# Seven block products for the up projections of a two-layer encoder, and one modulation computed in another place

## The chip, the cores and the metric

The kernel runs on one core of a Trainium2 chip. The core has engines with a queue of their own each: TensorE (PE, the matmuls; PEld is its loading of stationary operands), VectorE (DVE), ScalarE (ACT), GpSimd (POOL) and SyncE (SP), whose queue issues all transfers of this kernel. Matmul results land in PSUM, eight banks of 128 partitions x 512 float32; everything else lies in SBUF. The metric is the device time of one execution in microseconds (us), the median of several runs.

## The reference

Two sequences (a prompt of 256 tokens and a sample of 512) go through the same trunk of two layers, width 1024. Each layer has a mixer (layer 0: a matrix LSTM in both directions; layer 1: sliding-window attention) and a gated feed-forward with a convolution of three taps along the tokens. All of it is float32.

```python
for l in range(DEPTH):
    mod = jax.nn.silu(c) @ adaln_w[l] + adaln_b[l]          # 1024 -> 6 x 1024
    sh1, sc1, g1, sh2, sc2, g2 = [t[:, None, :] for t in jnp.split(mod, 6, axis=-1)]
    h = rmsnorm(x, norm_g[l, 0]) * (1 + sc1) + sh1
    y = mlstm_mixer(h, ...) if l % 2 == 0 else swa_mixer(h, ...)
    x = x + g1 * y
    h = rmsnorm(x, norm_g[l, 1]) * (1 + sc2) + sh2
    x = x + g2 * conv_ffn(h, ffn_w_up[l], ffn_conv_w[l], ffn_conv_b[l], ffn_w_down[l])
return rmsnorm(x, final_g)

def conv_ffn(h, w_up, conv_w, conv_b, w_down):
    u = h @ w_up                                            # 1024 -> 2 x 2816
    u = depthwise_conv3(u, conv_w) + conv_b
    return (jax.nn.silu(u[..., :2816]) * u[..., 2816:]) @ w_down
```

## The kernel before

Activations are kept transposed: channels on partitions (eight chunks of 128), the 768 tokens of both sequences on the free axis. Every float32 operand is split into a rounded high part and the rest (`fp_copy_split`, L166: ACT writes the high part at L170, DVE the low one at L171), and a product is three matmuls: high x high, high x low, low x high.

**Weights** come in units of 1 MB (`load`, L177), through two buffers with the tag `raw`; a unit is cut into two halves of 1024 columns, and each is split into `whi` and `wlo` (three buffers each). The matrices of the modulation come through the same two `raw` buffers.

**The program** is written in the order in which the work depends on each other, and a planner puts it on the queues: a list per engine, in which an instruction that isn't ready can be passed by a later one, and in which tiles of one tag take their buffers in turn. PSUM is three rotating banks `ps` (projections) and five rotating banks `pa` (norms, attention, down projections).

**Stages.** The first normalizations and layer 0's first modulation; mixer 0 (`mlstm`, L447), whose projections are followed by calls of `step` (L193); the output projection of the mixer with the residual (`out_proj`, L434), the sample's 512 tokens first and then the prompt's 256; feed-forward 0 (`ffn`, L834); mixer 1 (`swa`, L647); its output projection; feed-forward 1 with the final normalization.

**`step`** takes one piece from the generator `fill`. In mixer 0 this is a chain of the second and third part of layer 0's modulation (`adaln`, L292): eight pieces each, one transfer of 1 MB and its matmuls on PE to a piece. `step` is called once after the first window of mixer 0 (L218), after each of the seven further query and key projections, after the four value projections and after the four units of the output gate. A loop behind the mixer runs what is left. In feed-forward 0 `fill` is layer 1's modulation (`adaln_v`, L350): six groups of four transfers; for each transfer DVE makes four operations over 1024 columns that sum into one buffer `ada` (L364 and L366), and a group ends with four small matmuls with ones (they sum over the partitions), two copies and four transposes.

**A feed-forward** goes through 11 parts of 256 hidden channels. `up(p)` has two units (gate and value) of two halves; each half is 24 matmuls for the sample's 512 tokens and 24 for the prompt's 256 (`gemmT`). `conv` (L838) reads the result from PSUM: ACT does the middle tap with the bias (L841), DVE the outer two (L843, L844). Then Silu on ACT (L856), the product on POOL (L866), and the split of the product. `down(p)` runs after `up(p + 1)`: eight output chunks x two sequences x six matmuls into `pa`, and the residual update on DVE (L432).

**Norms** (`Norm`, L59) collect squares on ACT and their sum on POOL while the residual is updated; two later stages are put between other products by `tick`, and `ready` forces them. The first three halves of a feed-forward run as a `window`: one token range of 256 after the other, so that the products of the first ranges lie beside the norm of the last.

Of the kernel before, what the change touches and what calls it, by code (L numbers as in the profile page):

```python
# [13 lines left out]
P = 128  # L14
D = 1024
KC = D // P
T = 768
SEQS = ((0, 512), (512, 768))
# token ranges that are normalized on their own: (first, last, sequence)
SAMPLE, PROMPT = (0, 512, 0), (512, 768, 1)  # L20
RANGES = ((0, 256, 0), (256, 512, 0), PROMPT)
# [9 lines left out]
# column offsets inside the packed per-partition parameter block  # L31
# [11 lines left out]
# column offsets inside the block of shape constants  # L43
# [6 lines left out]
# weight unit indices  # L50
# [7 lines left out]

class Norm:  # L59
# [3 lines left out]
    def __init__(self, net, xt, rng, apply, pool_adds=True):  # L63
        self.net, self.xt, self.rng, self.apply = net, xt, rng, apply
# [16 lines left out]
    def stages(self):  # L81
# [17 lines left out]
        for c in range(KC):  # L99
            self.apply(c, self.x(c), pr, self.rng)  # L100
# [8 lines left out]
class Net:  # L109
    def __init__(self, tc, ctx, io):  # L110
# [8 lines left out]
        self.dp = pool("scratch", space=bass.MemoryType.DRAM)  # L119
        self.n = 0  # L120
# [26 lines left out]

    def ps(self):
        return self.psp.tile([P, 512], F32, tag="ps", name=self.nm("ps"), bufs=3)

    def pa(self):
        return self.psp.tile([P, 512], F32, tag="pa", name=self.nm("pa"), bufs=5)
# [13 lines left out]
    def fp_copy_split(self, hi, lo, src, scale=None):  # L166
        """hi = round(src * scale), lo = src * scale - hi"""
# [50 lines left out]
    def window(self, items):  # L218
        """several weight halves, one token range after the other"""
# [19 lines left out]
    def gemmN(self, u, evac):  # L239
        """tokens on partitions, 256 output columns on the free axis"""  # L240
# [15 lines left out]
    def setup(self):  # L256
# [19 lines left out]
        self.hh = self.hp.tile([P, KC, T], R, name="hh")  # L276
        self.hl = self.hp.tile([P, KC, T], R, name="hl")
# [72 lines left out]
    def adaln_v(self, l, pool):  # L350
        """the same with the sums over k of the rows of one partition on the vector engine"""
# [82 lines left out]
    def out_proj(self, u0, act, xt, l):  # L434
        for rng in (SAMPLE, PROMPT):
            norms = [Norm(self, xt, r, self.modulated(l, 1)) for r in RANGES if r[2] == rng[2]]
            for u in range(4):
                for h, w in self.halves(u0 + u):
                    c = 2 * u + h
                    self.resid(xt, self.gemmT(w, rng[2], act), l, 16, c, rng)  # L440
                    for n in norms:
                        n.square(c)
            for n in norms:
                self.start(n.rng, n.stages())

# [1 line left out]
    def mlstm(self, pool, gw, xt):  # L447
        nc, io = self.nc, self.io
        T6 = T // P
        # gates: rows 0-3 / 32-35 hold the forward / backward heads  # L450
# [57 lines left out]
        for h in range(4):  # L508
            # M along the free axis on all partitions, and its diagonal blocks masked
# [23 lines left out]
            # values, with two columns of ones for the normalizer  # L533
# [11 lines left out]
            # transposed scores: keys on partitions, queries on the free axis  # L545
# [86 lines left out]
        # output gate  # L632
# [14 lines left out]
    def swa(self, pool):  # L647
# [6 lines left out]
        def halves2(o, hh, ll, p0):  # L654
            """both partition halves of hh / ll from the 64 rows at p0"""
# [42 lines left out]
        # every row repeated, so that a row pitch of 511 reads it shifted by one per partition  # L698
# [135 lines left out]
    def ffn(self, l, xt, pool, apply, keep=None):  # L834
# [3 lines left out]
        def conv(ps, u, ch, s0, s1):  # L838
            n = s1 - s0
            w = lambda tap: self.cst(CW + (l * 44 + ch) * 3 + tap)  # L840
            nc.scalar.activation(u[:, s0:s1], ps, AF.Identity, bias=self.cst(CB + l * 44 + ch), scale=w(1))  # L841
            stt = nc.vector.scalar_tensor_tensor
            stt(u[:, s0 + 1 : s1], ps[:, : n - 1], w(0), u[:, s0 + 1 : s1], ALU.mult, ALU.add)  # L843
            stt(u[:, s0 : s1 - 1], ps[:, 1:], w(2), u[:, s0 : s1 - 1], ALU.mult, ALU.add)  # L844

        def up(p):
            g = self.slab([P, 2, 2, T], R)
            gs = {}

            def gate(c):  # L850
# [239 lines left out]
```

## Time and profile before

| | us |
|---|---|
| median of 3 runs | 1968.58 (1967.79 to 1971.22) |
| the profiled execution, from its first to its last instruction | 1968.9 |
| PE busy | 1890.1 |
| DVE busy | 1184.6 |
| ACT busy | 726.6 |
| POOL busy | 300.1 |
| moved by DMA | 188.63 MB, 96 GB/s on average |

A page of the profile gives busy times per engine, the span in slices, the chain of work that ended last, and the costliest groups of instructions. A group's row reads: line, engine, operation, what it writes <- what it reads, shape, number; then busy time in us and the mean of one in ns; then the idle time ahead of these on their engine and what ended it. In a timeline the first two numbers are start and duration in us. In a table of stretches each engine has its busy time and in brackets its instructions; the last three columns are the clock granted to PE, the share of DMA and GB/s. Matmuls overlap in PE's pipeline, so the duration of one is longer than the distance from one to the next.

### The profile page before, as it was taken

Reading aid. Unit: us, or ns where it says so; the run is one execution under the profiler, and the core shown is the slowest. Engines: PE = TensorE matmul, PEld = TensorE weight load, DVE = VectorE, ACT = ScalarE, POOL = GpSimd, SP = SyncE. Lnnn points to the kernel's source line nnn. Section 1 sums busy time; section 2 is a strip of 40 time slices with the busy share of each in tenths; the row PEclk is TensorE's granted clock in tenths of the full one; section 3 lists DMA queues with packets and bytes.
Section 4 is the critical chain, followed back from the end, with each engine's and each line's share of the span. In section 5 each row is a group of like instructions: output and inputs, shape, how many; then the busy total and the mean of one; then the engine's idle time right before and its main releaser. Section 6 shows DMA issues by size and latency. Waiting matters only on the chain.

```text
span 1968.9 us, 28848 instructions
## 1 busy us (share of the span) xinstructions
PE 1890.1 (96%) x11636; PEld 1638.4 (83%) x11636; DVE 1184.6 (60%) x2217; ACT 726.6 (37%) x1411; POOL 300.1 (15%) x336
## 2 busy tenths in 40 slices
PE   6799999999999999999999959999999999999997
PEld 2698898878988888888888858778988888888886
DVE  4534344323887778878556836785755555555556
ACT  3444344433442222222223526674532222222222
POOL 5111101223110000000002102243110000000003
PEclk9899999999999999999999979999999999999998
DMA  8313213243243233333112561123211111111111
GB/s 319 124 40 114 96 65 123 68 157 125 102 149 129 98 133 113 128 121 137 65 65 88 84 122 60 38 86 109 99 52 65 65 65 65 65 65 65 65 43 65
DMA packets 48609, 188.63 MB, mean 96 GB/s; under 512 B 3863, under 2 KB 21527, under 8 KB 33116
## 3 DMA queue, kind: packets, MB, share of 16 engines
q1 hardware_dynamic: 48476, 186.79, 28.7%
q8 instruction: 92, 1.51, 0.3%
q14 instruction: 41, 0.34, 0.1%
HBM read 176.17 MB, written 10.60 MB: 95 GB/s over the span
## 4 chain that ended last, share of the span: by engine, by line
PE 87%; DVE 5%; DMA 5%; ACT 1%; POOL 1%; issue 1%; SPq 0%; POOLq 0%; DVEq 0%; ACTq 0%
PE ps L164 58%; PE pa L164 27%; DMA bdiag<-bs 2%; PE pa L786 1%; DMA slab<-in_adaln_w_dram 1%; DMA raw<-in_adaln_w_dram 1%; DVE nt L404 1%; DVE ada L366 1%; POOL slab L418 1%; DVE hl L407 1%; DVE wlo L171 1%; POOL nt L79 1%; DVE slab L432 0%; ACT whi L170 0%; DMA bt<-bdiag 0%
## 5 line engine op out<-in xcount | busy, mean ns | idle before, releaser
L164 PE MATMUL ps<-hh,whi 128*128 128x256 f32 (+1 forms) x2096 | 697.4, 334 | 25.8 <-ACT vn L702 20.9
L164 PE MATMUL ps<-hl,whi 128*128 128x256 f32 (+1 forms) x2096 | 697.7, 333 | 0.3 <-DVE hl L171 0.3
L164 PE MATMUL ps<-hh,wlo 128*128 128x256 f32 (+1 forms) x2096 | 695.6, 333 | 1.0 <-DVE wlo L171 1.0
L164 PEld LDWEIGHTS ps<-hh,whi 128*128 128x128 f32 x2096 | 398.4, 191 | 75.3 <-ACT vn L702 21.3
L164 PEld LDWEIGHTS ps<-hh,wlo 128*128 128x128 f32 x2096 | 399.0, 190 | 40.1 <-DVE wlo L171 1.6
L164 PEld LDWEIGHTS ps<-hl,whi 128*128 128x128 f32 x2096 | 399.3, 191 | 38.3 <-DVE hl L171 0.5
L170 ACT CAST whi<-raw 128x1024 fp32r<-128x1024 f32 x208 | 215.9, 1049 | 455.3 <-PE ps L164 226.5
L164 PE MATMUL pa<-slab,whi 128*128 128x256 f32 (+1 forms) x1472 | 350.5, 333 | 0.4
L171 DVE TENSOR_TENSOR wlo<-raw,whi 128x1024 fp32r<-128x1024 f32 x208 | 256.7, 1244 | 155.0 <-ACT whi L170 141.1
L164 PEld LDWEIGHTS pa<-slab,whi 128*128 128x128 f32 x1472 | 250.9, 190 | 36.8 <-ACT whi L170 1.9
L432 DVE SCALAR_TENSOR_TENSOR slab<-pa,mod,slab 128x256 f32<-128x256 f32 (+1 forms) x368 | 215.1, 597 | 88.9 <-PE pa L164 88.2
L164 PE MATMUL pa<-slab,wlo 128*128 128x256 f32 (+1 forms) x736 | 239.9, 332 | 0.0
L866 POOL TENSOR_TENSOR uv<-uv,ug 128x768 f32<-128x768 f32 x44 | 81.3, 1847 | 966.6 <-DVE uv L844 966.6
L164 PEld LDWEIGHTS pa<-slab,wlo 128*128 128x128 f32 x736 | 139.6, 191 | 14.1
L366 DVE SCALAR_TENSOR_TENSOR ada<-raw,silc,ada 128x1024 f32<-128x1024 f32 x84 | 108.6, 1327 | 16.9 <-DMA raw<-in_adaln_w_dram 16.6
L79 POOL TENSOR_TENSOR nt<-nt,nt 128x256 f32<-128x256 f32 x105 | 89.4, 860 | 159.0 <-ACT nt L78 154.9
L170 ACT CAST slab<-uv 128x768 fp32r<-128x768 f32 x44 | 36.7, 835 | 182.8 <-POOL uv L866 182.8
L841 ACT ACTIVATE ug<-ps,cstt 128x512 f32<-128x512 f32 x84 | 56.7, 675 | 104.5 <-PE ps L164 104.5
L843 DVE SCALAR_TENSOR_TENSOR ug<-ps,cstt,ug 128x511 f32<-128x511 f32 x84 | 51.9, 618 | 69.5 <-ACT ug L841 69.4
L843 DVE SCALAR_TENSOR_TENSOR uv<-ps,cstt,uv 128x511 f32<-128x511 f32 (+1 forms) x86 | 52.8, 614 | 57.3 <-ACT uv L841 57.3
L164 PE MATMUL pa<-slab,slab 128*128 128x256 f32 (+2 forms) x336 | 72.5, 342 | 7.1 <-ACT slab L170 7.1
L778 POOL TENSOR_SCALAR t<-t,st 128x256 f32<-128x256 f32 (+1 forms) x96 | 50.2, 535 | 181.2 <-DVE st L776 96.0
(175 smaller groups left out, 2172.7 us busy)
## 6 DMA issues: line engine op xcount, KB each, us to landing
raw<-in_w_dram SPq DMA_DIRECT2D x104, 1024.0 KB, 4.8
raw<-in_adaln_w_dram SPq DMA_DIRECT2D x40, 1024.0 KB, 5.1
slab<-in_x_dram SPq DMA_DIRECT2D x12, 512.0 KB, 9.4
slab<-in_adaln_w_dram SPq DMA_DIRECT2D x12, 512.0 KB, 10.2
bdiag<-bs SPq DMA_DIRECT2D x1, 4096.0 KB, 44.4
slab<-mrows SPq DMA_DIRECT2D x8, 384.0 KB, 5.8
xs<-slab SPq DMA_DIRECT2D x6, 512.0 KB, 2.9
bt<-bdiag SPq DMA_DIRECT2D x16, 192.0 KB, 2.7
```

What stands on the lines that cost most here:

```text
L79: self.add(self.acc, self.acc, sq, ALU.add)
L164: self.nc.tensor.matmul(out, lhsT, rhs, start=start, stop=stop)
L170: nc.scalar.copy(hi, src)
L171: nc.vector.tensor_tensor(lo, src, hi.bitcast(F32), ALU.subtract)
L366: stt(acc[:, s], raw[:, i], w, acc[:, s], ALU.mult, ALU.add)
L404: nc.vector.scalar_tensor_tensor(t, x, self.gain[l][i][:, c, q : q + 1], pr, ALU.mult, ALU.mult)
L407: nc.vector.scalar_tensor_tensor(lo, t, sh, hi.bitcast(F32), ALU.add, ALU.subtract)
L432: self.nc.vector.scalar_tensor_tensor(x, o, self.mod[l][:, gc + c, q : q + 1], x, ALU.mult, ALU.add)
L778: nc.gpsimd.tensor_scalar(t[:, e, :K], t[:, e, :K], rd[:, e : e + 1], 1.0, ALU.mult, ALU.mult)
L841: nc.scalar.activation(u[:, s0:s1], ps, AF.Identity, bias=self.cst(CB + l * 44 + ch), scale=w(1))
L843: stt(u[:, s0 + 1 : s1], ps[:, : n - 1], w(0), u[:, s0 + 1 : s1], ALU.mult, ALU.add)
L866: nc.gpsimd.tensor_tensor(u, u, gs[c], ALU.mult)
```

## The change

**Seven products.** For a unit of 256 up channels (two blocks of 128 outputs), the 1024 inputs are cut into two blocks of 512 and the 768 tokens into two of 384, which makes a product of 2 x 2 by 2 x 2 blocks. Instead of eight block products seven are made (Strassen's scheme in Winograd's form). Each is 4 chunks x 3 matmuls of 384 columns (`quarters`).

- The token side needs seven operands. `combined` makes them from the normalized activations, once per feed-forward: B11 and B21 from the first 384 tokens; from the second 384 B22 and the sums and differences N1, N2, T3, T4, each split into high and low.
- The weight side needs four sums over 512 columns for each unit, on POOL (`pair`), and splits of 3 x 1024 + 512 columns for each unit instead of 2 x 1024.
- The products are summed in four fixed banks a, e, b, d. ACT copies a running sum from one bank into another, on which PE goes on summing; four sums of 384 columns per part remain for DVE. The result lies in SBUF (`urow`, `yrow`), with a gap of four zeros between the sequences, and the convolution runs over both sequences at once, from SBUF. The second output block comes with its sign turned, and `ncw` holds the turned taps.
- PSUM is now four banks `pa` and four others, which rotate in the mixers and are fixed in the feed-forwards (`banks`). The output projections run over two halves of 384 tokens. The prompt comes first in the layout. The window at the start of a feed-forward is replaced by the products of the first two pairs that need only the first 384 tokens.

**Layer 1's modulation** (`adaln_v`, unchanged) is third in mixer 0's `fill` instead of feed-forward 0's; the calls of `step` in the feed-forward are gone, those in mixer 0 are as before. The buffer of the scratch for dynamic DMA is set to 1024.

```diff
+    def banks(self, fixed):
+        with self.tc.tile_pool(name="ps", bufs=1, space=bass.MemoryType.PSUM) as self.pb:
+            self.bank = [self.pb.tile([P, 512], F32, name=self.nm("ps")) for _ in range(4)] if fixed else None
+            yield
     def pa(self):
-        return self.psp.tile([P, 512], F32, tag="pa", name=self.nm("pa"), bufs=5)
+        return self.psp.tile([P, 512], F32, tag="pa", name=self.nm("pa"), bufs=4)
...
+    def combined(self, l, i, pool):
...
+        def apply(c, x, pr, rng):
...
+            k = c - 4
+            b12, b22, b11, b21 = held[k], b, full[k], full[c]
+            n1, n2, t3, t4 = b11, self.tmp([P, H]), b12, b21
+            nc.gpsimd.tensor_tensor(n1, b11, b12, ALU.subtract)
+            put(self.N1, k, n1)
+            nc.gpsimd.tensor_tensor(t3, b22, b12, ALU.subtract)
+            nc.vector.scalar_tensor_tensor(n2, n1, -1.0, b22, ALU.mult, ALU.subtract)
+            put(self.N2, k, n2)
+            nc.vector.scalar_tensor_tensor(t4, n2, -1.0, b21, ALU.mult, ALU.subtract)
+            put(self.T3, k, t3)
+            put(self.T4, k, t4)
+            for z in range(2):
+                self.b22[z][k] = one(R)
+            put(self.B22, k, b22)
...
+    def quarters(self, o, w, j, start):
+        hi, lo = self.quarter(j)
+        wh, wl = (t.rearrange("p (k m) -> p k m", k=4) for t in w)
+        mm = self.nc.tensor.matmul
+        for k in range(4):
+            mm(o, wh[:, k], hi[k], start=start and k == 0, stop=False, skip_group_check=True)
+            mm(o, wh[:, k], lo[k], start=False, stop=False, skip_group_check=True)
+            mm(o, wl[:, k], hi[k], start=False, stop=k == 3, skip_group_check=True)
+        self.tick(2.1)
+
+    def pair(self, pool, u, bank, rows):
...
+        raw = self.load(u)
+        q = [raw[:, 512 * i : 512 * (i + 1)] for i in range(4)]
+        s1 = pool.tile([P, 512], F32, tag="s1", name=self.nm("s1"), bufs=1)
+        add = lambda o, x, y: nc.gpsimd.tensor_tensor(o, x, y, ALU.add)
+        add(s1, q[2], q[3])
+        wa = self.split(raw[:, :1024])
+        add(q[2], q[2], q[0])
...
+        self.quarters(a, part(wa, 0), self.B11, True)
...
+        add(q[0], q[0], s1)
+        self.fp_copy_split(s1h, s1l, s1)
+        add(q[1], q[1], q[0])
+        wc = self.split(raw[:, :1024])
+        wb = self.split(raw[:, 1024:])
+        nc.scalar.copy(b, fork)
+        self.quarters(e, (s1h, s1l), self.N1, True)
+        self.quarters(b, part(wc, 0), self.N2, False)
+        if u1 is None:
+            self.quarters(a, part(wa, 1), self.B21, False)
+        nc.scalar.copy(d, b)
+        p5 = self.tmp([P, H])
+        nc.scalar.copy(p5, e)
+        self.quarters(d, part(wb, 0), self.T3, False)
...
+        u3 = self.tmp([P, H])
+        nc.scalar.copy(u3, d)
+        self.quarters(b, part(wc, 1), self.B22, False)
+        nc.vector.tensor_tensor(r2[:, col(H) :], e, u3, ALU.add)
+        self.quarters(d, part(wb, 1), self.T4, False)
+        nc.vector.tensor_tensor(r1[:, col(H) :], b, p5, ALU.add)
...
-            if p == 0:
-                first = [next(items) for _ in range(3)]
-                self.window([(w, f(c)) for f, c, w in first])
...
+            if first:
+                for x in pairs:
+                    next(x)
+                self.ready(HALVES[0])
...
+                for x in pairs[::-1]:
+                    next(x)
+                self.ready(HALVES[1])
...
-        self.fill = chain(self.adaln(0, 1), self.adaln(0, 2))
-        with tc.tile_pool(name="mlstm", bufs=1) as pool:
-            act = self.mlstm(pool, gates, xt)
-            for _ in self.fill:
-                pass
...
-        with tc.tile_pool(name="ffn0", bufs=1) as pool:
-            self.fill = self.adaln_v(1, pool)
-            self.ffn(0, xt, pool, self.modulated(1, 0), xs)
...
+        self.fill = chain(self.adaln(0, 1), self.adaln(0, 2), self.adaln_v(1, pool))
+        act = self.mlstm(pool, gates, xt)
+        for _ in self.fill:
+            pass
+        return act
```

More of the change, by code (lines that the diff above doesn't have):

```diff
@@ L1 @@
+from contextlib import contextmanager
 import numpy as np
@@ L98, in stages @@
         net.mm(pr, net.ones, dg, True, True)
-        for c in range(KC):
+        for c in self.order:
             self.apply(c, self.x(c), pr, self.rng)
@@ L432, in resid, with out_proj @@
         self.nc.vector.scalar_tensor_tensor(x, o, self.mod[l][:, gc + c, q : q + 1], x, ALU.mult, ALU.add)
-    def out_proj(self, u0, act, xt, l):
-        for rng in (SAMPLE, PROMPT):
-            norms = [Norm(self, xt, r, self.modulated(l, 1)) for r in RANGES if r[2] == rng[2]]
+    def out_proj(self, u0, act, xt, l, apply):
+        for half in HALVES:
+            c0, c1, _ = half
+            norm = Norm(self, xt, half, apply, order=PAIRED)
             for u in range(4):
```

214 lines of the change are left out of this document (149 added, 65 removed).

## The prediction

> **What bounds the kernel now.** I read the page first, then the busy time by stretches of 100 us, then single places in the timelines.
>
> ```profile
> span 1968.9 us, 28848 instructions
> PE 1890.1 (96%) x11636; PEld 1638.4 (83%) x11636; DVE 1184.6 (60%) x2217; ACT 726.6 (37%) x1411; POOL 300.1 (15%) x336
> PE 87%; DVE 5%; DMA 5%; ACT 1%; POOL 1%; issue 1%; SPq 0%; POOLq 0%; DVEq 0%; ACTq 0%
> 200.00:300.00 100.00, 99.29 (x685) 88.70 (x684) 41.92 (x97) 39.08 (x108) 8.34 (x13) 1.00 0.26 90
> 600.00:700.00 100.00, 99.97 (x569) 86.78 (x568) 78.63 (x106) 28.49 (x36) 5.55 (x3) 1.00 0.36 127
> 1500.00:1600.00 100.00, 100.00 (x576) 87.97 (x575) 55.93 (x80) 28.49 (x37) 7.37 (x4) 1.00 0.19 64
> ```
>
> PE is full in mixer 0 (200 to 300), in feed-forward 0 (600 to 700) and in feed-forward 1 (1500 to 1600), and 87% of the chain of waits is PE. So matmuls taken away are worth their cadence, as long as nothing else has become late. DVE has room in mixer 0 (42%) and in feed-forward 1 (56%), little in feed-forward 0 (79%), where it works out layer 1's modulation.
>
> **Strassen's matmuls.** The cadence comes from two runs of 24 matmuls, first and last of each:
>
> ```profile
> 400.71 0.40 PE L164 MATMUL ps<-hh,whi 128*128 128x512 f32 x1
> 405.95 0.39 PE L164 MATMUL ps<-hh,wlo 128*128 128x512 f32 x1
> ...
> 406.17 0.28 PE L164 MATMUL ps<-hh,whi 128*128 128x256 f32 x1
> 408.93 0.28 PE L164 MATMUL ps<-hh,wlo 128*128 128x256 f32 x1
> ```
>
> 23 steps in 5.24 us are 0.228 us for 512 columns, 23 in 2.76 are 0.120 for 256; half way, 384 columns take 0.174. A part of a feed-forward (256 hidden channels) has 4 halves x 2 sequences x 24 = 192 up matmuls of 384 columns on average; seven products of 12 for each of 2 units are 168, all of 384. The 24 saved are 4.2 us a part, 22 parts: **-92 us**. A part was 288 matmuls, 50 us (576 in the 100 us at 1500), and would be 45.8.
>
> **What the vector engines get for it.** Rows, mean ns behind the bar's busy time:
>
> ```profile
> L171 DVE TENSOR_TENSOR wlo<-raw,whi 128x1024 fp32r<-128x1024 f32 x208 | 256.7, 1244 | 155.0 <-ACT whi L170 141.1
> L170 ACT CAST whi<-raw 128x1024 fp32r<-128x1024 f32 x208 | 215.9, 1049 | 455.3 <-PE ps L164 226.5
> L432 DVE SCALAR_TENSOR_TENSOR slab<-pa,mod,slab 128x512 f32<-128x512 f32 x160 | 118.3, 747 | 44.8 <-PE pa L164 44.7
> L432 DVE SCALAR_TENSOR_TENSOR slab<-pa,mod,slab 128x256 f32<-128x256 f32 x208 | 97.7, 482 | 44.1 <-PE pa L164 43.6
> L366 DVE SCALAR_TENSOR_TENSOR ada<-raw,silc,ada 128x1024 f32<-128x1024 f32 x84 | 108.6, 1327 | 16.9 <-DMA raw<-in_adaln_w_dram 16.6
> L171 DVE TENSOR_TENSOR slab<-uv,slab 128x768 fp32r<-128x768 f32 x44 | 41.9, 953 | 48.2 <-ACT slab L170 48.2
> L866 POOL TENSOR_TENSOR uv<-uv,ug 128x768 f32<-128x768 f32 x44 | 81.3, 1847 | 966.6 <-DVE uv L844 966.6
> L79 POOL TENSOR_TENSOR nt<-nt,nt 128x256 f32<-128x256 f32 x105 | 89.4, 860 | 159.0 <-ACT nt L78 154.9
> L790 ACT COPY pt<-pa 128x384 f32<-128x384 f32 x16 | 7.6, 473 | 4.6 <-PE pa L786 4.5
> ```
>
> DVE for a part: a unit is split as 3 x 1024 and 512 columns instead of 2 x 1024, so 2 x (3 x 1.244 + 0.75) + 2 x 1.244 for the down unit = 11.4 us; the convolution's eight operations over 771 columns, read from SBUF, lie between 0.747 (512) and 1.327 (1024), say 1.04: 8.3; the split of the gated product 2 x 0.953 = 1.9; four sums of 384 at 0.61 (between 0.482 and 0.747): 2.5; the residual 8 x (0.747 + 0.482) = 9.8. Together 33.9 us of 45.8. POOL gets eight sums of weights, 512 columns, about 1.3 each between its rows of 256 and 768, and keeps two products: 14.1 us. ACT gets 4.2 us more of splits (4 x 1.049) and some 16 copies of PSUM (0.473 for 384): it was 14.2 a part and is about 22. No engine is over PE, but DVE and POOL are not independent:
>
> ```profile
> 545.05 1.85 POOL L866 TENSOR_TENSOR uv<-uv,ug 128x768 f32<-128x768 f32 x1 [21.59 <-DVE uv L844]
> 545.52 3.65 DVE L366 SCALAR_TENSOR_TENSOR ada<-raw,silc,ada 128x1024 f32<-128x1024 f32 x2 [0.64 <-DMA raw<-in_adaln_w_dram]
> L366 DVE SCALAR_TENSOR_TENSOR ada<-raw,silc,ada x84: 1270/1278/2520, 520.1 to 929.1; 128x1024 f32<-128x1024 f32 x84
> L432 DVE SCALAR_TENSOR_TENSOR slab<-pa,mod,slab x368: 468/485/754, 584.3 to 1953.9; 128x256 f32<-128x256 f32 x104, 128x512 f32<-128x512 f32 x80
> ```
>
> Two DVE operations that take 1.28 us each (minimum/median/maximum 1270/1278/2520 ns) took 3.65 when they met a POOL product: the first stood until POOL's end at 546.90. Operations with one operand in PSUM (L432) never went over 754 ns. So of a part's 33.9 us, the 21.6 with both operands in SBUF (11.4 + 8.3 + 1.9) exclude POOL's 14.1. The sum lies between 33.9 us (POOL runs under the PSUM work) and 48.0 (every POOL operation stops DVE). Feed-forward 0 ran without a gap at 79% DVE; here it will be near 90%. The waits that could then show on PE are the ACT copies between products (0.473 against 2.1 us of the product that runs meanwhile, hidden), the splits behind POOL's sums, and the four `pa` banks of `down` (five before) when residuals are late. I take 1.15 us of stall a part, between 0 and 3.7 (no gain left of the 4.2 but 0.5): **+25 us**.
>
> The Trainium skill, "SBUF — State Buffer", section "SBUF: two separate sides", says that the shared port pair is an exclusive lock for DVE operations with two SBUF inputs against GpSimd operations that read SBUF, and that the loser fully blocks. The trace agrees (2520 against 1278 ns). By the rule alone a part would tend to 48.0 us; by the row of a saturated but gapless feed-forward 0 it stays at 45.8.
>
> **Layer 1's modulation.** It leaves feed-forward 0, where its small matmuls took PE time:
>
> ```profile
> L164 PE MATMUL ps<-ada,ones 128*32 128x512 f32 x40 | 6.4, 605 | 0.0
> L379 PE MATMUL ps<-kct,nt 128*128 128x128 f32 x20 | 3.2, 272 | 0.0
> ```
>
> These are five of the six groups (580 to 940 us): 9.6 us, so **-11 us** for six. Where it goes is the main point. The generator is put third in the chain of `fill`. Mixer 0 calls `step` 1 + 7 + 4 + 4 = 16 times, and the two generators before it yield 8 times each. So nothing of it is asked for until the loop at the end of the mixer, where all 24 transfers and their 96 DVE operations are asked for at once, ahead of the output projection. They use the same two `raw` buffers as all weights:
>
> ```profile
> 437.73 1.06 PE L164 MATMUL ps<-raw,silc 128*32 128x512 f32 x6
> ...
> 392.41 0.33 SPq L312 DMA_DIRECT2D raw<-in_adaln_w_dram  x1
> 397.83 0.33 SPq L179 DMA_DIRECT2D raw<-in_w_dram  x1
> 411.46 0.33 SPq L312 DMA_DIRECT2D raw<-in_adaln_w_dram  x1
> 419.77 0.33 SPq L179 DMA_DIRECT2D raw<-in_w_dram  x1
> ...
> 439.58 0.71 PE L164 MATMUL ps<-slab,whi 128*128 128x512 f32 x2
> ...
> raw<-in_w_dram SPq DMA_DIRECT2D x104, 1024.0 KB, 4.8
> raw<-in_adaln_w_dram SPq DMA_DIRECT2D x40, 1024.0 KB, 5.1
> L364 DVE TENSOR_SCALAR ada<-raw,silc 128x1024 f32<-128x1024 f32 x12 | 8.9, 787 | 0.0
> ```
>
> Weight transfers wait for nothing but a buffer, yet they stand in the queue in the order in which the program asks: the sixteenth modulation transfer at 411.46, and only then, at 419.77, the first of the output projection, whose first matmul is at 439.58. In the new kernel 24 transfers come between these. DVE needs 108.6 + 8.9 = 117.5 us for them. With two buffers a turn is one transfer (5.1, and 0.25 of hand-over), since DVE's four operations (4 x 1.28) end just before. A group is a first turn of 4.2 us, three of 5.35, and 2.4 while the one sum buffer is read by four matmuls of 0.605: 22.7 us. The second buffer is free only about 439 (the six matmuls at 437.73 that read it are PE's last in the mixer), so the first group ends near 454.6, the last at 454.6 + 5 x 22.7 = 568. The projection's first transfer follows the 23rd turn, at 563; 4.8 us to land and 2.3 to split (1.049 + 1.244) put its first matmul at 570. Nothing else is left for PE: all later work hangs on the projection, and the fixed banks take the place of the mixer's rotating ones, which the last group still uses. **+130 us**, between 105 (DVE's 117.5 us without a pause from 425 on) and 150 (5 us between groups).
>
> **The start of each feed-forward.** Before, little is lost there:
>
> ```profile
> 520.00:530.00 10.00, 7.86 (x65) 7.60 (x63) 9.14 (x19) 5.07 (x11) 0.71 (x1) 1.00 0.32 107
> 530.00:540.00 10.00, 9.68 (x69) 9.69 (x70) 5.31 (x11) 2.51 (x5) 0.00 (x0) 0.83 0.00 0
> 550.00:560.00 10.00, 9.71 (x55) 8.24 (x54) 9.02 (x12) 3.09 (x5) 1.85 (x1) 1.00 0.32 105
> ```
>
> 2.8 us idle. After, the last normalization covers 384 tokens instead of 256, and `combined` makes five more operands of it: per pair of chunks nine DVE operations of about 0.61 us (5.5) and two POOL differences of 1.0, which mostly stop DVE: 6.5 us, four times 26. With 6.5 us ahead of it (last residual, square, sum, the row sums, the power) the last operand is there some 32 us after the projection's last matmul. PE meanwhile has four products of the first half (4 x 12 x 0.174 = 8.4 us) and two that can follow the operands as they come (4.2). So 20 us idle, 17.5 more than before, at both layers: **+35 us**, between 10 (the operands come as fast as PE takes them) and 50.
>
> **Small ones.** Four `pa` banks instead of five in both mixers: 0 to 15, taken as +3. The clock that was granted fell to 0.83 for 10 us after a short stop (530 to 540), 1.7 us lost: one stop more, +2. The new sign, gap and layout operations are a handful, off the path.
>
> **Sum.** 1968.9 - 92 - 11 + 130 + 35 + 25 + 3 + 2 = 2061; the profiled span stands 0.3 us over the median of the runs. I forecast **2060 us**, slower.
>
> **Rivals.**
> 1. The modulation is hidden: its transfers are interleaved with the mixer's weights after all, or the projection's overtake them. Then the 130 us fall away: 1930, faster. For it: DVE is 42% busy in mixer 0 and 117.5 us fit into it; it decides if less than 39 us of the 130 remain. Against it: the order in the queue above and the count of the steps. 10%.
> 2. DVE and POOL together bound the parts: 49.5 us instead of 47, 55 us more: 2115. For it: 48.0 us when they never overlap; against: a third of DVE's work reads PSUM and can run under POOL. 15%.
> 3. Only the modulation costs: no stall in the parts, and the operands keep up, so 25 and 30 us fall away: 2005. For it: feed-forward 0 ran gapless at 79%; against: the 26 us of operands have little cover. 15%.
> 4. The forecast, 60%, with a range of its own of 2030 to 2090.
>
> **Numbers.** The range is 1995 to 2120: the forecast, the third rival and the second; the first is left out. What can be told from no change is 0.2%, about 4 us. Faster 0.11 (the first rival and a tail of the third), same 0.01, slower 0.88.
>
> **What would show it.** A stretch of some 130 us after mixer 0 in which PE is idle and DVE does L366's operation without pause, with 24 modulation transfers in a row on the queue; parts of about 47 us; idle PE of about 20 us ahead of each feed-forward, ended by DVE's splits; DVE near 90% in the parts, with many operations at twice their median. I am wrong if modulation transfers alternate with weights before the end of the mixer, or if the parts take 49 us or more.

## The result and the profile after

| | before | after |
|---|---|---|
| median | 1968.83 us (1967.79 to 1971.22, 4 runs) | 2055.84 us (2051.69 to 2059.41, 4 runs) |
| ratio | | 1.0438 [1.0421, 1.0455] |
| span of the profiled execution | 1968.9 us | 2057.5 us |

The change makes the kernel 87 us slower; 2060 was forecast, in a range of 1995 to 2120. From the page of the changed kernel:

```profile
span 2057.5 us, 28177 instructions
PE 1845.5 (90%) x10964; PEld 1649.4 (80%) x10964; DVE 1389.6 (68%) x2256; ACT 911.0 (44%) x1805; POOL 617.9 (30%) x514
PE 67%; DVE 16%; DMA 7%; issue 4%; ACT 3%; POOL 3%; SPq 0%; POOLq 0%; DVEq 0%; ACTq 0%
```

PE does 672 matmuls less and 44.6 us less work, but it is 90% busy instead of 96%, and a third of the chain is no longer PE. To see where, both spans are cut at the same marks: the last residual of an output projection, and the first and the last down matmul of a feed-forward. The stretches are: up to the end of output projection 0; start of feed-forward 0; its parts; mixer 1 with its output projection; start of feed-forward 1; its parts. Before:

```profile
0.00:513.10 513.10, 480.23 (x3015) 404.80 (x3016) 223.01 (x444) 207.90 (x473) 102.43 (x118) 0.98 0.35 124
513.10:579.80 66.70, 63.74 (x407) 58.21 (x407) 57.31 (x80) 27.29 (x42) 10.19 (x10) 0.97 0.35 119
579.80:1087.50 507.70, 505.34 (x2951) 440.60 (x2950) 372.90 (x524) 148.95 (x203) 49.61 (x38) 1.00 0.31 108
1087.50:1393.80 306.30, 282.03 (x1988) 239.43 (x1988) 202.79 (x667) 170.41 (x462) 73.73 (x121) 0.96 0.34 86
1393.80:1462.30 68.50, 66.33 (x433) 61.27 (x431) 40.61 (x67) 29.08 (x44) 11.78 (x10) 0.98 0.22 76
1462.30:1953.50 491.20, 489.16 (x2843) 432.17 (x2842) 279.10 (x417) 141.76 (x187) 46.95 (x36) 1.00 0.17 58
```

and after (second column: length of the stretch; then PE, PEld, DVE, ACT, POOL; the third from the end is the granted clock):

```profile
0.00:621.40 621.40, 491.75 (x3054) 412.55 (x3054) 347.56 (x568) 211.24 (x483) 116.49 (x120) 0.90 0.41 143
621.40:705.00 83.60, 70.47 (x331) 62.90 (x332) 61.68 (x76) 49.01 (x86) 37.27 (x25) 0.82 0.15 51
705.00:1178.50 473.50, 462.90 (x2654) 433.24 (x2653) 354.28 (x430) 216.94 (x347) 168.79 (x110) 1.00 0.21 71
1178.50:1486.30 307.80, 283.84 (x1954) 243.25 (x1952) 204.49 (x667) 171.14 (x464) 87.62 (x123) 0.96 0.34 85
1486.30:1571.30 85.00, 71.87 (x330) 64.31 (x331) 61.68 (x76) 49.01 (x86) 37.10 (x25) 0.81 0.14 50
1571.30:2043.00 471.70, 461.80 (x2638) 431.63 (x2637) 351.32 (x422) 212.76 (x338) 165.91 (x110) 1.00 0.18 63
```

So +108.3 us before feed-forward 0, +16.9 and +16.5 at the starts, -34.2 and -19.5 in the parts, +1.5 in mixer 1; with -0.9 behind the last part this is the whole difference of 88.6. Feed-forward 1 as a whole, where no modulation ever ran, went from 559.7 to 556.7 us: the seven products brought 3 us there, of 46 that the missing matmuls are worth.

**Behind mixer 0.** Four views of the changed kernel in one window: PE's timeline (the mixer's last matmuls, the projection's first), SP's, the waits of PE, and the operations on the sum buffer (minimum/median/maximum in ns, first and last start).

```profile
418.24 1.07 PE L200 MATMUL ps<-raw,silc 128*32 128x512 f32 x8
...
548.60 0.59 PE L200 MATMUL ps<-slab,whi 128*128 128x384 f32 x2 [0.47 <-DVE mod L428]
```

```profile
424.03 110.25 SPq L401 DMA_DIRECT2D raw<-in_adaln_w_dram  x21
539.48 49.86 SPq L215 DMA_DIRECT2D raw<-in_w_dram  x8
```

```profile
PE ps L200 <- DVE ada L408: 96.5, 6, 17.0
```

```profile
L408 DVE SCALAR_TENSOR_TENSOR ada<-raw,silc,ada x84: 1269/1279/2315, 408.3 to 543.0; 128x1024 f32<-128x1024 f32 x84
L200 PE MATMUL ps<-ada,ones x48: 1030/1061/1062, 436.1 to 545.2; 128*32 128x512 f32 x48
```

The last 21 of the 24 modulation transfers stand in one row ahead of the output projection's first weights, which follow at 539.48. PE waits six times for the sums, 96.5 us in all. From the end of the mixer's last product (418.24 + 1.07 = 419.31) to 548.60 are 129.3 us. The chain shows a group's period (its rows are start, duration, what):

```profile
436.14 3.14 PE ps L200 x8
...
521.59 3.05 PE ps L200 x8
```

Four groups in 85.45 us, 21.4 each.

**The start of feed-forward 0.** Stretches of 10 us, waits of PE from 620 to 700, and two matmuls of one product.

```profile
640.00:650.00 10.00, 4.98 (x10) 2.25 (x9) 10.00 (x15) 6.15 (x13) 4.74 (x5) 0.50 0.00 1
650.00:660.00 10.00, 6.67 (x15) 4.30 (x16) 9.28 (x15) 4.89 (x11) 4.06 (x4) 0.50 0.01 2
670.00:680.00 10.00, 10.00 (x59) 9.90 (x58) 7.37 (x7) 6.74 (x10) 6.83 (x4) 1.00 0.09 39
```

```profile
PE ps L962 <- DVE zl L207: 6.1, 7, 1.5
PE ps L961 <- ACT zh L206: 6.0, 4, 4.0
```

```profile
658.80 0.52 PE L962 MATMUL ps<-zl,whi 128*128 128x384 f32 x1
...
662.00 0.52 PE L963 MATMUL ps<-zh,wlo 128*128 128x384 f32 x1
```

DVE is full for 20 us, and PE takes the operands one by one: 25 matmuls in 20 us against 59 in 10. It does so at half its clock: ten steps in 3.20 us are 0.32 us for 384 columns, where the prediction's cadence was 0.174. Whole stretch: 13.1 us of 83.6 without a matmul (before 3.0 of 66.7), and a clock of 0.82 over the 70.5 busy ones, worth 12.7 (before 0.97 over 63.7, 1.9). As a count of PE's time that is 21 of the 25 us of loss (16.9 longer with 48 matmuls, 8.3 us, fewer); it names no cause, since a slow clock costs nothing where PE would wait for the next operand anyway. The Trainium skill, "TensorE: Matmul & The Clock Gate", part 1 ("The HAM clock gate"), says that PE falls to half its clock after an idle window of about 3.4 us and comes back only after as long a busy one; the trace agrees, since the 0.50 follows a wait of 4.0 us and lasts as long as matmuls only trickle; full steps are back at 662.33, 4.0 us after the last wait.

What holds the start is seen in four more lines: the norm's last sum on POOL, its row sums on PE, and the first and the last operation of `combined` on DVE.

```profile
623.79 2.02 POOL L103 TENSOR_TENSOR nt<-nt,nt 128x384 f32<-128x384 f32 x1
629.10 0.72 PE L200 MATMUL pa<-inv,nt 128*128 128x2 f32 x6
634.15 1.13 DVE L927 SCALAR_TENSOR_TENSOR nt<-slab,gain,pa 128x384 f32<-128x384 f32 x2
657.81 1.50 DVE L207 TENSOR_TENSOR bq<-nt,bq 128x384 fp32r<-128x384 f32 x1
```

The operations on the operands take from 634.15 to 659.31, 25.2 us. By then PE has done the four products of the first half and two more, and from 658.32 on it hardly waits until the first down matmul at 704.96. But the projection's last matmul ended at 617.54, so 16.6 us go by before the first of these operations (17.7 in layer 1). In them the last residual stands behind a weight split on DVE (until 621.39), the norm's last sum behind two sums of weights on POOL (until 623.79), and the row sums, whose input is there at 625.81, behind products on PE (until 629.10). The clock's own price is small by comparison: ten matmuls from 621.52 on, ahead of the row sums, and twelve from 658.32 on took 7.4 us instead of 3.8 at 0.174, which makes some 3.5 us, an estimate from the timeline.

**The parts.** The stretch of seven parts of feed-forward 0, PE's waits in it, the first matmuls of the second and the tenth down projection, and a meeting of POOL and DVE.

```profile
760.00:1096.00 336.00, 328.80 (x1850) 308.44 (x1850) 247.91 (x281) 153.52 (x239) 116.74 (x71) 1.00 0.20 67
```

```profile
PE ps L963 <- DVE wlo L207: 3.6, 5, 0.8
```

```profile
753.78 0.62 PE L200 MATMUL pa<-slab,whi 128*128 128x512 f32 x2
...
1136.49 0.86 PE L200 MATMUL pa<-slab,whi 128*128 128x512 f32 x3
```

```profile
902.41 1.86 POOL L1063 TENSOR_TENSOR slab<-slab 128x772 f32<-128x772 f32 x1 [4.41 <-DVE slab L1033]
```

```profile
903.08 2.27 DVE L207 TENSOR_TENSOR wlo<-raw,whi 128x1024 fp32r<-128x1024 f32 x1 [0.82 <-ACT whi L206]
```

A part takes (1136.49 - 753.78) / 8 = 47.8 us, against 50.2 before (feed-forward 1). DVE is 74% busy (247.91 of 336), not near 90%. The split at 903.08 stands while POOL multiplies, as was said (the rule of the Trainium skill that the prediction weighed, "SBUF — State Buffer", section "SBUF: two separate sides", holds); what that is worth is for an experiment to say.

### The profile page after: what moved, and what is told of

Same layout as the page of the kernel before. It is cut to its first block, busy times and chain, and to the rows that moved or that the text cites. A ratio compares the mean times of both kernels' runs of the same rounds, so it can differ in the third digit from the quotient of the medians.

```text
span 2057.5 us, 28177 instructions
## 1 busy us (share of the span) xinstructions
PE 1845.5 (90%) x10964; PEld 1649.4 (80%) x10964; DVE 1389.6 (68%) x2256; ACT 911.0 (44%) x1805; POOL 617.9 (30%) x514
## 4 chain that ended last, share of the span: by engine, by line
PE 67%; DVE 16%; DMA 7%; issue 4%; ACT 3%; POOL 3%; SPq 0%; POOLq 0%; DVEq 0%; ACTq 0%
PE ps L200 21%; PE pa L200 19%; PE ps L963 9%; PE ps L961 8%; PE ps L962 8%; DVE wlo L207 3%; DVE ada L408 3%; DMA raw<-in_adaln_w_dram 3%; DMA bdiag<-bs 2%; DVE slab L474 2%; PE pa L842 1%; ACT whi L206 1%; DVE slab L1032 1%; DVE slab L207 1%; DVE slab L1033 1%
## 5 line engine op out<-in xcount | busy, mean ns | idle before, releaser
L200 PE MATMUL ps<-zh,whi 128*128 128x256 f32 (+2 forms) x688 | 228.7, 336 | 22.1 <-ACT whi L206 15.9
L200 PE MATMUL ps<-zh,wlo 128*128 128x256 f32 (+2 forms) x688 | 229.7, 335 | 3.1 <-DVE wlo L207 3.1
L200 PE MATMUL ps<-zl,whi 128*128 128x256 f32 (+2 forms) x688 | 230.1, 335 | 0.1
L961 PE MATMUL ps<-zh,whi 128*128 128x384 f32 x528 | 183.1, 347 | 7.0 <-ACT zh L206 3.2
L963 PE MATMUL ps<-zh,wlo 128*128 128x384 f32 x528 | 181.1, 343 | 8.9 <-DVE wlo L207 8.9
L962 PE MATMUL ps<-zl,whi 128*128 128x384 f32 x528 | 181.2, 343 | 6.3 <-DVE zl L207 6.3
L200 PEld LDWEIGHTS ps<-zh,whi 128*128 128x128 f32 x688 | 131.9, 193 | 37.8 <-ACT whi L206 17.5
L200 PEld LDWEIGHTS ps<-zh,wlo 128*128 128x128 f32 x688 | 132.2, 192 | 14.6 <-DVE wlo L207 4.0
L200 PEld LDWEIGHTS ps<-zl,whi 128*128 128x128 f32 x688 | 132.2, 192 | 10.9 <-issue 1.7
L974 POOL TENSOR_TENSOR raw<-raw 128x512 f32<-128x512 f32 x88 | 131.5, 1495 | 6.4
## 6 DMA issues: line engine op xcount, KB each, us to landing
slab<-in_adaln_w_dram SPq DMA_DIRECT2D x12, 512.0 KB, 10.3
```

The lines of the kernel that those rows point to most:

```text
L200: self.nc.tensor.matmul(out, lhsT, rhs, start=start, stop=stop)
L961: mm(o, wh[:, k], hi[k], start=start and k == 0, stop=False, skip_group_check=True)
L962: mm(o, wh[:, k], lo[k], start=False, stop=False, skip_group_check=True)
L963: mm(o, wl[:, k], hi[k], start=False, stop=k == 3, skip_group_check=True)
L974: add = lambda o, x, y: nc.gpsimd.tensor_tensor(o, x, y, ALU.add)
```

## The experiments

Theory at the outset: the loss is the order of the transfers through the two `raw` buffers, with DVE's chain of operands at the starts and small stalls in the parts. Rivals: the fixed banks or DVE's work for the modulation hold mixer 0's end; POOL's lock on DVE holds the parts. Ratios are to the kernel before, in runs beside it.

**1. The kernel before, with the modulation moved as in the change.**

```diff
-            self.fill = self.adaln_v(1, pool)
...
+            self.fill = chain(self.adaln(0, 1), self.adaln(0, 2), self.adaln_v(1, pool))
```

> The kernel before, with nothing of the seven products and its rotating banks (3 ps, 5 pa), but with layer 1's modulation third in mixer 0's fill (and the scratch at 1024, which makes room for its sum buffer). If the order of the raw buffers makes the stall: 1969 + 120 to 130 - 11 (its small matmuls leave feed-forward 0) = 2078 to 2088 us. If the fixed banks that take the mixer's place make it: within 1950 to 1975 us.

2083.82 us, 1.0581 [1.0565, 1.0597]. Its queue of SP, and the waits of PE from 430 to 570:

```profile
442.23 109.85 SPq L359 DMA_DIRECT2D raw<-in_adaln_w_dram  x21
556.85 41.28 SPq L179 DMA_DIRECT2D raw<-in_w_dram  x6
```

```profile
PE ps L164 <- DVE ada L366: 95.8, 6, 16.9
```

The same row of 21 transfers and the same wait, with no seven products and no fixed banks in the kernel. The place of the modulation in the program, and with it the order of the transfers, is the cause, and by itself it costs 114 us here (1969.80 for the kernel before in runs beside it).

**2. The kernel before, with the PSUM banks as the changed kernel has them in the mixers.**

```diff
-tag="ps", name=self.nm("ps"), bufs=3)
+tag="ps", name=self.nm("ps"), bufs=4)
...
-tag="pa", name=self.nm("pa"), bufs=5)
+tag="pa", name=self.nm("pa"), bufs=4)
```

> The kernel before with four ps and four pa banks instead of three and five, nothing else. In the changed kernel mixer 0 ended 19 us earlier than before and mixer 1 was 5 us shorter. If the fourth ps bank does that: 1940 to 1950 us. If it comes from the order of the sequences (prompt first): 1965 to 1975 us.

1948.41 us, 0.9897 [0.9883, 0.9912]: faster than both kernels. The first 100 us of the kernel before, and of this one:

```profile
0.00:100.00 100.00, 68.47 (x393) 47.01 (x394) 48.51 (x95) 39.87 (x77) 32.53 (x45) 0.90 0.59 219
```

```profile
0.00:100.00 100.00, 76.99 (x465) 55.05 (x466) 51.00 (x98) 41.83 (x81) 34.80 (x46) 0.95 0.58 219
```

With a fourth `ps` bank PE gets through 72 more matmuls in the first 100 us. Its mixer 0 ends at 419.1 us, as the changed kernel's does; with three banks it ended at 438.8 (six matmuls from 437.73 on, shown in the prediction). The fifth `pa` bank isn't missed. So the +108.3 us up to the end of output projection 0 are 129.3 of stall, less 19.5 for that bank, and 1.5 less for the projection and the 0.8 us ahead of it before.

**3. More calls of `step`.** One more call for each key block of the scores in mixer 0, 24 in all, so that the modulation is asked for during the mixer:

```diff
+                    self.step()
```

> The changed kernel with one more call of step ahead of each of the 24 key blocks of mixer 0's scores, so that the 24 pieces of layer 1's modulation are asked for one by one inside the mixer. If the 129 us between mixer 0's last product (419 us) and the output projection's first matmul (549 us) come from 24 transfers asked for at once through two raw buffers, nearly all of it goes: 2056 - 129 + up to 15 for weights that now wait behind a modulation transfer, 1927 to 1942 us, faster than before. If instead the 117 us of DVE work have no room in the mixer, or the change of PSUM pools is what holds the projection, most of the time stays: over 2000 us.

2018.96 us, 1.0257 [1.024, 1.0274]: a miss, the modulation isn't hidden. SP's queue in the mixer:

```profile
222.61 69.34 SPq L401 DMA_DIRECT2D raw<-in_adaln_w_dram  x7
298.44 0.34 SPq L215 DMA_DIRECT2D raw<-in_w_dram  x1
```

Seven modulation transfers take 69 us, ten for each, since a buffer comes free only when DVE has done four operations between the mixer's own work; and the mixer's next weights stand behind them. The output projection now starts at 512.5 instead of 548.6. The stall has moved into the mixer and lost a third.

**4. Three pieces for each call,** in the 16 places that there were:

```diff
-        next(self.fill, None)
+        for _ in range(3):
+            next(self.fill, None)
```

> The changed kernel with three pieces of fill per call of step instead of one, at the 16 places it had. The stall behind the mixer goes as in the run with one piece at 40 places, but each weight unit now stands behind three transfers that each keep a buffer for some 5 us of DVE: if the two raw buffers are what counts, PE waits some us per unit in the mixer, 1940 to 1975 us. If only the number of pieces left at the end counts, it is as fast as the other: 1927 to 1942 us.

1997.26 us, 1.0142 [1.0127, 1.0157]: slower than either forecast. Pieces in threes cost less than those of run 3 (the projection starts at 487.9), but that is still 68.6 us behind 419.3, where the changed kernel's mixer ends. PE's longest wait from 150 to 490 is not for weights: it is for the mixer's own chain through POOL (`hs`, 35.2 us in four waits), and of the 95 us from 205 to 300 the chain that ended last has 47 on DVE, where operations of the modulation and of the mixer take turns. So DVE's order costs here too, and not only the turns of the two buffers.

**5. Run 3 with the modulation's sums on PE** (the small matmuls of `adaln`, as layer 0 has them), which leaves DVE free and gives a buffer back sooner:

```diff
-        self.fill = chain(self.adaln(0, 1), self.adaln(0, 2), self.adaln_v(1, pool))
+        self.fill = chain(*(self.adaln(*z) for z in ((0, 1), (0, 2), (1, 0), (1, 1), (1, 2))))
```

> The changed kernel with 40 single pieces in mixer 0 as in the first experiment, but layer 1's modulation by layer 0's generator (sums on PE: 24 transfers, four matmuls each, buffer free as soon as PE has read it) instead of the one that keeps a raw buffer for 5 us of DVE. If what slowed the mixer is how long a modulation transfer holds one of the two raw buffers: 2056 - 129 + 24 x 0.5 us of matmuls + some 10 us, 1935 to 1955 us. If it is the number of transfers in the queue (24 MB more) or the projections' waiting behind any transfer: over 1985 us.

1991.82 us, 1.0117 [1.0095, 1.0138]. A stretch of its mixer and its waits of PE from 150 to 490:

```profile
150.00:200.00 50.00, 42.17 (x245) 28.93 (x244) 16.64 (x41) 18.12 (x48) 5.30 (x5) 0.87 0.56 203
```

```profile
PE ps L200 <- DMA raw<-in_adaln_w_dram: 13.8, 6, 3.0
```

DVE is at a third here (16.64 of 50), and PE still waits for transfers. So DVE was a part of what made the modulation dear in mixer 0 (27 us between run 3 and this one), but not all of it. The mixer's products end at 483.2 instead of 419.3, 64 us later. A piece takes PE 0.99 us in the chain, twice what was expected, which makes 24 us; the waits are 24 us; the rest, some 16, fits the granted clock of 0.94 over 315.6 busy us from 150 to 490.

**6. Half the POOL work of the parts away:** three of the four sums in `pair`.

```diff
-        add(q[2], q[2], q[0])
...
-        add(q[0], q[0], s1)
...
-        add(q[1], q[1], q[0])
```

> The changed kernel with three of the four weight sums of a unit left out (POOL from 16.7 to about 8 us a part; the products run on the unsummed weights, so this leaves out part of the computation). If the exclusion of DVE by POOL makes the low parts of the weights late, the parts go from 48.05 to 46.0 to 46.8 us and the splits' mean on DVE from 1.33 towards 1.23 us; over 22 parts 28 to 45 us. If the stalls come from DVE's or ACT's own queues, the parts stay at 47.5 to 48 us.

2047.54 us (one run). The convolution's outer tap in the changed kernel and here, and the seven parts here (760 to 1096, as above):

```profile
L1032 DVE SCALAR_TENSOR_TENSOR slab<-slab,ncw,slab 128x771 f32<-128x771 f32 x14 | 20.7, 1478 | 2.3 <-ACT slab L1030 2.3
```

```profile
L1029 DVE SCALAR_TENSOR_TENSOR slab<-slab,ncw,slab 128x771 f32<-128x771 f32 x15 | 15.2, 1016 | 6.1 <-ACT slab L1027 6.1
760.00:1096.00 336.00, 331.06 (x1869) 312.40 (x1868) 231.13 (x286) 153.62 (x240) 48.36 (x28) 1.00 0.19 66
```

The lock is real: the tap falls from 1478 to 1016 ns, and DVE has 16.8 us less to do in seven parts (247.91 - 231.13). The splits of the weights, for which the expectation was made, keep their mean of 1331 ns. But a part is shorter by only some 0.4 us: the first-to-last times of the parts go from 473.5 and 471.7 to 469.3 and 467.2. What POOL takes from DVE is mostly time that DVE had to spare.

**7. The order of the operands.** N1 as the norm delivers, then N2 and T3, T4 and B22 last; once with N1 and T3 on POOL as in the change, once on DVE:

```diff
-            nc.gpsimd.tensor_tensor(n1, b11, b12, ALU.subtract)
...
+                nc.vector.tensor_tensor(full[c], full[c], b, ALU.subtract)
...
+            nc.vector.tensor_tensor(held[k], b, held[k], ALU.subtract)
```

> The changed kernel with the operands of the second half made in another order: N1 of all four chunks first, then N2 and T3 chunk by chunk, T4 and B22 last, so that PE can start each product earlier; the same instructions otherwise (one buffer less). From the end of the output projection to the first down matmul it was 87.5 us (layer 0) and 88.7 (layer 1). If the order makes PE wait: 80 to 84 us each. If the whole chain of DVE work is what bounds, because PE needs B22 and T4 anyway: 86 to 89.

> As the run before, and the eight differences n1 and t3 on DVE instead of POOL: eight more DVE operations (about 5 us), no exclusion by POOL and no crossing to another engine. If POOL's operations stop DVE there: 3 to 5 us shorter than the run before at each feed-forward's start. If they run beside DVE: 3 to 5 us longer.

2058.98 and 2055.56 us (one run each). The starts take 84.3 and 85.6 us in the new order with POOL, 80.8 and 82.0 on DVE, against 83.6 and 85.0 in the changed kernel. The order gives nothing, since PE has to wait for the whole chain; eight POOL differences less give 3.5 us a start. Both totals lie within the spread of the changed kernel's own runs, so this rests on the starts alone (run 10, whose starts are those of the changed kernel, has 82.5 and 83.8, so that about 1 us is spread).

**8. The low halves of T3, T4 and B22 left out,** twelve DVE operations of a start:

```diff
+            if j in (self.T3, self.T4, self.B22):
+                nc.scalar.copy(hi[k], src)
```

> The changed kernel without the low halves of the operands T3, T4 and B22 (their high half is read twice instead: part of the computation is left out, no matmul is): twelve DVE operations of 0.6 to 0.9 us fewer at each feed-forward's start. From the projection's last residual to the first down matmul it was 83.6 us (layer 0) and 85.0 (layer 1). If DVE's chain bounds the start: 75 to 77 each. If ACT, POOL or the crossings between them bound it: 81 to 85.

2046.98 us (one run); the starts take 77.4 and 77.7 us. DVE has 10.3 us less to do in a start (51.4 instead of 61.7), and the starts lost 6.2 and 7.3. So DVE's chain holds the start, but not one for one: what is left of the 10.3 is held elsewhere, and the run doesn't show where.

**9. The split weights in six buffers of 512 columns** instead of three of 1024, the same bytes:

```diff
-        hi = self.stg.tile([P, 1024], R, tag="whi", name=self.nm("whi"), bufs=3)
-        lo = self.stg.tile([P, 1024], R, tag="wlo", name=self.nm("wlo"), bufs=3)
+            his.append(self.stg.tile([P, 512], R, tag="whi", name=self.nm("whi"), bufs=6))
+            los.append(self.stg.tile([P, 512], R, tag="wlo", name=self.nm("wlo"), bufs=6))
```

> The changed kernel with the split weights in six buffers of 512 columns each instead of three of 1024 (same memory, twice as many and half as long operations of ACT and DVE), so that a buffer comes free after one product and not after the later of two. If the stalls inside the parts come from splits that wait for one of three buffers: parts 46.3 to 46.8 us instead of 48.05, 2020 to 2035 us. If DVE's own queue makes the low parts late, the shorter operations cost more than they give: 2050 to 2070 us.

2038.94 us, 1.0353 [1.0336, 1.037]. The seven parts, the second and the tenth down projection, and the splits in these parts:

```profile
760.00:1096.00 336.00, 335.97 (x1914) 318.82 (x1912) 266.43 (x347) 161.89 (x300) 128.30 (x74) 1.00 0.19 66
```

```profile
746.15 0.62 PE L221 MATMUL pa<-slab,whi 128*128 128x512 f32 x2
...
1118.30 0.62 PE L221 MATMUL pa<-slab,whi 128*128 128x512 f32 x2
```

```profile
L228 DVE TENSOR_TENSOR wlo<-raw,whi 128x512 fp32r<-128x512 f32 x116 | 96.9, 845 | 38.0 <-ACT whi L227 37.9
```

PE is busy for 335.97 of 336 us, and a part takes 46.5, although DVE works more than before (79%, 1024 columns in two operations of 845 ns instead of one of 1331). The stall in the parts came from the three coarse buffers, not from DVE's throughput: in the changed kernel ACT's casts wait 65.1 us of the 336 for PE to give such a buffer back. The run halves the operations along with the buffers, so that a half that is ready sooner may have its part; this isn't told apart. The two feed-forwards are 8.2 and 12.5 us shorter (548.9 and 544.2).

**10. The modulation on PE, a third in mixer 0 and two thirds in mixer 1,** behind whose start they can be spread:

```diff
-        self.fill = chain(self.adaln(0, 1), self.adaln(0, 2), self.adaln_v(1, pool))
+        self.fill = chain(self.adaln(0, 1), self.adaln(0, 2), self.adaln(1, 0))
...
+                    mods = [self.adaln(1, 1), self.adaln(1, 2)]
+                    self.fill = (None for m in mods for _ in m)
```

> The changed kernel with layer 1's modulation on PE (layer 0's generator), its first third (shift and scale of mixer 1) as eight single pieces in mixer 0, the other two thirds in mixer 1, where PE stands 15 us before the bias transfer. Eight pieces instead of 24 between mixer 0's weights: a third of that experiment's 64 us, and some 10 us in mixer 1: 1945 to 1965 us, faster than before. If mixer 1 pays for its pieces as mixer 0 did: 1975 us or more.

1975.27 us (10 runs), 1.0031 [1.0021, 1.004]. Mixer 0 keeps its length nearly (output projection 0 ends at 508.9 us, 112 earlier than in the changed kernel), but mixer 1 with its projection grows from 307.8 to 340.1, which takes back more than was expected.

**11. Runs 7 (on DVE), 9 and 10 together.**

> The three edits that took something back, put together: layer 1's modulation as small matmuls on PE, a third in mixer 0 and two thirds in mixer 1 (split_mod), operand sums on DVE in phases (phases_dve), split weights in six buffers of 512 columns (fine). If they work in different places, their gains against the changed kernel add up: split_mod stands at 1975, fine took 17 us, phases_dve 3.5 us at each of two starts measured against the same order with POOL, but nothing to 3 us in all against the changed kernel: 1948 to 1960, 0.99 to 0.995 of the kernel before, and feed-forward starts of 70 to 74 us. If fine and phases_dve work on the same wait (the first half's weights waiting for buffers while the operands are made), only the larger counts: starts of 74 to 75 us, 1956 to 1962. If the finer buffers make more instructions late in the mixers, where the modulation now goes through the same two raw buffers: 1965 or more.

1943.5 us (1941.7 to 1945.75), 0.9872 [0.9855, 0.9888]. Three of its stretches (mixer 1, start and parts of feed-forward 1):

```profile
1050.70:1387.20 336.50, 306.42 (x2084) 247.15 (x2082) 212.14 (x702) 174.46 (x495) 78.07 (x121) 0.96 0.45 125
1387.20:1458.00 70.80, 56.32 (x272) 51.97 (x272) 59.07 (x88) 43.74 (x85) 32.23 (x15) 0.83 0.13 45
1458.00:1927.00 469.00, 465.30 (x2686) 441.51 (x2686) 368.20 (x504) 226.60 (x424) 171.28 (x110) 1.00 0.19 66
```

The gains add up, and a little more than that. (The start's 70.8 us can't be set against the 85.0 of the changed kernel: they hold 272 matmuls, not 330, because a down product comes earlier.) Feed-forward 1 is down to 539.8 us, 4.4 less than in run 9 alone and 19.9 less than before. Of that, mixer 1 takes back 30.2 (336.5 against 306.3) for 128 matmul instructions of the modulation and 6 us more of idle PE. From the kernel before with four `ps` banks (run 2) this version can hardly be told apart: 0.9872 against 0.9897, with intervals that overlap, on two chips. What is sure of its gain could be had by that one bank.

## Why the prediction came out right

The forecast of 2061 for the profiled execution stands against 2057.5. The steps, in its order:

- **Strassen's matmuls, -92.** The size was right where nothing else holds: a part without stalls takes 46.5 us (run 9) against 50.2 before, 3.7 of the 4.2.
- **The vector engines, +25.** The total of a part was close, 47.8 against 47; its reason was wrong. DVE is at 74%, not near 90%, and POOL's lock is worth about 0.4 us of a part (run 6). The stall, 1.3 us against run 9, was the three `whi`/`wlo` buffers, which the prediction counted among "the splits behind POOL's sums" and did not look at as buffers. ACT's load was put at 22 us a part, though the terms given for it add up to 26; 21.9 were measured (153.52 in seven parts).
- **Layer 1's modulation, -11 and +130.** The term that decides, and right in place, cause and size: 129.3 us, 24 transfers in the queue ahead of the projection's weights, DVE's operation without pause. A group took 21.4 us, not 22.7, although its small matmuls took 1.06 us (0.605 was taken); and the mixer ended earlier than assumed. Shown by run 1 without the rest of the change. The 11 us are seen too: feed-forward 0 gained 14.3 us more than feed-forward 1 (17.3 against 3.0).
- **The starts, +35.** Undersized: 25 us each, 50 in all, instead of 17.5. The chain of DVE operations was the right mechanism (run 8) and had the right size, 25.2 us for 26, and PE does six products meanwhile, as was said. The step that failed is the "6.5 us ahead of it (last residual, square, sum, the row sums, the power)": 16.6 and 17.7 us lie between the projection's last matmul and the first operation of the chain, because these links stand behind splits and sums of weights and behind products on three engines. The clock was put at 2 us for the whole kernel; by the estimate above it costs some 3.5 at a start.
- **The banks, +3.** Wrong in sign: -19.5. Only the lost `pa` bank was weighed; that `ps` went from three to four in the mixers stood in the change and wasn't priced (run 2).

So the total is good because errors cancel, which is luck: some 23 us too many up to the end of output projection 0, 9.7 and 13.0 too few in the feed-forwards.

Of the rivals, the second fails (a part 47.8 us, not 49.5, and DVE has room). The third fails (the two starts cost 50 us, where it has 5, and a part has its stall of 1.3). The first would have been true for no order tried in mixer 0 (runs 3 to 5). Its argument was that 117.5 us of DVE fit into mixer 0; in runs 3 and 4 the modulation's operations on DVE, its transfers and the mixer's own work hold each other up, and with DVE free of it (run 5) the two `raw` buffers and PE's own part still cost 64 us. Not tried: a third `raw` buffer, or a buffer of the modulation's own. Nor is there a run of the seven products with layer 1's modulation left in feed-forward 0; feed-forward 1, which has none, stands for it.

## What to carry to other kernels

A stream that can wait costs nothing only if it doesn't hold a resource that an urgent stream needs next; so count, for each shared buffer and queue, what will stand ahead of the next weights, before counting engine time. Fewer matmuls are worth their cadence only where the operands come as fast as before; ask of the first operand on which engines each link ahead of it will stand in line, and don't add up the links as if the engines were free. Count rotating buffers and PSUM banks in both directions: one bank more gave 20 us, and the same bytes in six pieces instead of three took away the stalls of the parts.

## What the runs showed of the hardware

- PE's granted clock was 0.50 in a stretch in which matmuls came singly, as operands were ready (640 to 660 us, 25 matmuls). 384 columns took 0.32 us there, 0.174 at full clock. In the burst behind mixer 0 (granted clock 0.56 from 420 to 548) the small matmuls with 512 columns took 1.06 us instead of 0.605.
- A DVE operation of 512 columns takes 845 ns on average in run 9, one of 1024 takes 1331: halving costs 27% more DVE time, and still made the kernel 17 us faster.
- POOL's work makes DVE's operations longer by up to half on average (1478 against 1016 ns), which with DVE at 74% moved the time by less than 1%.
